# The down projection in seven-product form over pairs of token tiles, with its weight combinations stored ahead

## The chip, the cores and the metric

The kernel runs on one core of one Trainium2 chip. The metric is the device time of one execution in microseconds. Five engines of the core matter here. TensorE (PE in the profile) multiplies 128x128 blocks. VectorE (DVE) and GpSimd (POOL) do elementwise arithmetic. ScalarE (ACT) does activations, copies and casts, and issues some transfers. SyncE (SP) only issues transfers. Each engine takes its own instructions strictly in order and waits on semaphores for the others.

## The reference

Two layers' worth of input, 2048 prompt rows and 8 x 16 sample rows, go through one layer: a normalised input projection, a gated-delta group and a short-convolution group, an output projection, and then the feed-forward block that the change is about. With `D_MODEL` 1024 and `D_FF` 2816 it is

```
h = rmsnorm(x, norm_ffn_pre)
f = (silu(h @ w_gate) * (h @ w_up)) @ w_down
x = x + rmsnorm(f, norm_ffn_post)
```

All tensors are float32. The 2176 rows are 17 tiles of 128 rows, tile 16 being the sample rows. `D_FF` is 22 blocks of 128 (`NF`).

## The kernel before

**Split products.** A matmul operand is a reduced float32 type (`F32R`). To keep precision, each operand is split in two: `hi`, the cast of the value, made by ACT, and `lo`, the value minus `hi`, made by DVE or POOL. A product is then three matmuls: hi x hi, hi x lo, lo x hi.

**Stages.** The program has four stages: the input projection with the two mixers, the output projection (`o_tile`), gate/up, and the down projection.

**Gate/up** (L740 to L893). The tiles are taken in three groups (`FGROUPS`: 6, 6 and 5 tiles); each group runs over all 22 column blocks f. It already has a seven-product form (Winograd's variant of Strassen's scheme): the two rows of blocks are gate and up, the two inner halves are the halves of `D_MODEL`, and the two columns are the halves of the group's tokens. Seven products of half the size take the place of eight. `ffn_load` fetches the group's activations from `hTd`; `ffn_prep` makes the seven combinations of activations and splits them (28 pairs `xh`, `xl`). `gu_weights` makes the seven weight tiles of one column block: in group 0 it loads `rg` and `ru`, forms the four sums S1 to S4 on DVE, splits all seven, and stores the four split sums in DRAM (`fsplit`); in groups 1 and 2 it splits only the three plain quarters and fetches the four stored ones. The tiles `fw` are a ring of 12 (`NWB`). `gate_up` runs the seven products, combines them on DVE, POOL and ACT, and stores the result in `actd`, one DRAM tensor for each group and chunk of column blocks.

**Down** (L896 to L957). The 22 blocks are cut into four chunks (`FCHUNKS`: 6, 6, 5, 5). At the start of a chunk `down_weights` loads each block of `w_dn`, casts it on ACT and splits it on POOL. Then `down_tile` runs for each of the 17 tiles: load the tile's part of `actd`, split it (ACT, DVE), multiply it by the chunk's weights into two PSUM banks of 512 columns, and add these to the tile's accumulator `acc[t]` (ACT copies in the first chunk, DVE adds after that). In the last chunk it also squares, normalises, adds the residual `x2d` and stores `y`.

**Order.** The program is written in loops, but the instructions of each engine are put in order by a scheduler that runs a time model of its own while the kernel is built; within one engine that order is then fixed. So a piece of work written after another can come before it, and work of different loops is interleaved.

## Time and profile before

| | |
|---|---|
| median of 3 runs | 2717.77 us (2716.97 to 2719.88) |
| profiled execution | 2717.92 us, span 2716.1 us |
| granted TensorE clock, mean | 0.98 |
| gate/up, group 0 / seam / group 1 / seam / group 2 | from 1258.6 / 1566.7 / 1614.5 / 1895.0 / 1926.0 us |
| entry to the down projection | 2182.5 to 2222.4 us |
| down projection | 2222.4 to 2707.6 us |
| after the last matmul | 2707.6 to 2716.1 us |
| DMA traffic | 561.03 MB, mean 207 GB/s |

The page of the profile gives busy time by engine, the chain of work that ended last, and groups of instructions (line, engine, operation, output <- inputs, size, count | busy us, mean ns of one | idle time before them and what ended it). A table by windows gives for each stretch the length, each engine's busy time with its number of instructions, the granted clock, the DMA share and GB/s. Matmuls overlap in the record, so what one costs in a dense stretch is the stretch divided by the count, not the mean duration. Waiting for a memory port is inside an instruction's recorded duration; waiting for a semaphore is idle time before it.

### The profile page before, as it was taken

The numbers are of one execution on the slowest core, as the hardware profiler recorded it, in microseconds if no ns is written. First come the engines' busy times: TensorE is split into PE (matmuls) and PEld (weight loads), VectorE is DVE, ScalarE is ACT, GpSimd is POOL, SyncE is SP. The second block draws the span as 40 slices with busy tenths as digits, with TensorE's granted clock in tenths as the row PEclk, the third lists the DMA queues.
The fourth block names the chain that finished last, engine by engine and source line by source line (L and its number), as shares of the span: only waits on it lengthen the run. The fifth ranks groups of instructions, "written<-read, shape, count | busy, mean of one in ns | idle before, by whom it ended". The sixth has DMA issues, their size and how long they took to land.

```text
span 2716.1 us, 41011 instructions
## 1 busy us (share of the span) xinstructions
PE 2586.1 (95%) x15369; PEld 2402.7 (88%) x15369; DVE 1412.3 (52%) x3008; ACT 882.0 (32%) x2013; POOL 686.1 (25%) x601
## 2 busy tenths in 40 slices
PE   5789999999999999998999999999999989999998
PEld 4679989899998997877999989999999978888887
DVE  7877656575675656677655562222522221223366
ACT  3424143151423404343444442223433232211122
POOL 2231000010000101124655563444644440201000
PEclk9889999999999999998999999999999999999999
DMA  8887665656666574767766677777788841212144
GB/s 296 297 300 260 221 219 199 227 187 223 216 211 212 185 232 135 233 220 248 270 238 248 243 239 223 229 227 222 229 268 256 257 170 51 95 46 67 49 149 167
DMA packets 255541, 561.03 MB, mean 207 GB/s; under 512 B 48508, under 2 KB 137280, under 8 KB 233840
## 3 DMA queue, kind: packets, MB, share of 16 engines
q1 hardware_dynamic: 162800, 494.93, 54.6%
q10 hardware_dynamic: 92544, 63.49, 7.4%
q8 instruction: 121, 1.98, 0.3%
q14 instruction: 76, 0.62, 0.1%
HBM read 416.74 MB, written 141.60 MB: 206 GB/s over the span
## 4 chain that ended last, share of the span: by engine, by line
PE 51%; DVE 2%; POOL 1%; DMA 1%; issue 1%; ACT 0%; POOLq 0%; ACTq 0%; DVEq 0%
PE fbank L843 31%; PE ybank L936 18%; PE tbank L708 1%; PE dbank L708 1%; DVE xl L781 1%; DMA dr<-in_w_dn 1%; POOL dl L911 0%; DVE fh L775 0%; DVE fh L772 0%; POOL xl L781 0%; POOL fw L822 0%; PE ftbank L730 0%; DMA fh<-hTd 0%; DMA x2d<-xo 0%; POOL ft L766 0%
## 5 line engine op out<-in xcount | busy, mean ns | idle before, releaser
L843 PE MATMUL fbank<-xh,fw 128*128 128x384 f32 (+1 forms) x3696 | 899.1, 326 | 3.5 <-ACT fw L821 2.0
L131 PE MATMUL dbank<-hi,w 128*128 128x384 f32 (+1 forms) x2688 | 704.7, 341 | 36.2 <-POOL w L292 10.7
L843 PEld LDWEIGHTS fbank<-xh,fw 128*128 128x128 f32 x3696 | 652.3, 188 | 5.5 <-ACT fw L821 2.4
L843 PE MATMUL fbank<-xl,fw 128*128 128x384 f32 (+1 forms) x1848 | 604.0, 327 | 10.2 <-DVE xl L781 10.2
L131 PEld LDWEIGHTS dbank<-hi,w 128*128 128x128 f32 x2688 | 493.5, 196 | 49.2 <-POOL w L292 14.1
L131 PE MATMUL dbank<-lo,w 128*128 128x384 f32 (+1 forms) x1344 | 453.6, 338 | 0.0
L843 PEld LDWEIGHTS fbank<-xl,fw 128*128 128x128 f32 x1848 | 347.7, 188 | 13.2 <-DVE xl L781 13.0
L936 PE MATMUL ybank<-dh,ah 128*128 128x512 f32 x748 | 289.4, 392 | 6.7 <-ACT ah L926 6.7
L936 PE MATMUL ybank<-dh,al 128*128 128x512 f32 x748 | 291.9, 391 | 0.9 <-DVE al L927 0.9
L936 PE MATMUL ybank<-dl,ah 128*128 128x512 f32 x748 | 291.6, 390 | 0.0
L131 PEld LDWEIGHTS dbank<-lo,w 128*128 128x128 f32 x1344 | 264.0, 196 | 2.3 <-issue 0.2
L822 POOL TENSOR_TENSOR fw<-rg,fw 128x512 fp32r<-128x512 f32 x132 | 182.8, 1385 | 238.5 <-ACT fw L821 238.5
L936 PEld LDWEIGHTS ybank<-dh,ah 128*128 128x128 f32 x748 | 141.3, 189 | 36.7 <-ACT ah L926 7.4
L936 PEld LDWEIGHTS ybank<-dh,al 128*128 128x128 f32 x748 | 141.0, 188 | 31.2 <-DVE al L927 2.0
L941 DVE TENSOR_TENSOR acc<-acc,ybank 128x512 f32<-128x512 f32 x102 | 69.9, 685 | 188.8 <-PE ybank L936 188.6
L936 PEld LDWEIGHTS ybank<-dl,ah 128*128 128x128 f32 x748 | 141.0, 189 | 29.4 <-POOL dl L911 0.2
L870 DVE TENSOR_TENSOR u<-m,fbank 128x384 f32<-128x384 f32 (+1 forms) x66 | 35.0, 530 | 238.6 <-PE fbank L843 238.6
L927 DVE TENSOR_TENSOR al<-ar,ah 128x768 fp32r<-128x768 f32 (+1 forms) x68 | 75.1, 1107 | 128.3 <-ACT ah L926 128.3
L821 ACT CAST fw<-rg 128x512 fp32r<-128x512 f32 x132 | 82.3, 624 | 163.9 <-PE fbank L843 155.0
L926 ACT CAST ah<-ar 128x768 fp32r<-128x768 f32 (+1 forms) x68 | 53.2, 785 | 253.1 <-PE ybank L936 251.3
L317 DVE SCALAR_TENSOR_TENSOR acc<-R,cw,acc 128x384 f32<-128x384 f32 (+1 forms) x216 | 129.6, 604 | 1.6
L911 POOL TENSOR_TENSOR dl<-dr,dh 128x1024 fp32r<-128x1024 f32 x22 | 53.6, 2443 | 254.2 <-ACT dh L910 251.7
(292 smaller groups left out, 3560.2 us busy)
## 6 DMA issues: line engine op xcount, KB each, us to landing
w<-wsplit SPq DMA_DIRECT2D x140, 1024.0 KB, 5.0
fw<-fsplit SPq DMA_DIRECT2D x176, 512.0 KB, 4.4
fsplit<-fw SPq DMA_DIRECT2D x88, 512.0 KB, 3.0
rg<-in_w_gu SPq DMA_DIRECT2D x66, 512.0 KB, 4.2
wsplit<-w SPq DMA_DIRECT2D x28, 1024.0 KB, 5.1
actd<-at ACTq DMA_DIRECT2D x44, 384.0 KB, 4.9
wr<-in_w_in SPq DMA_DIRECT2D x56, 256.0 KB, 5.7
ar<-actd SPq DMA_DIRECT2D x34, 384.0 KB, 3.1
```

The costliest lines, as they stand in the source:

```text
L131: T.matmul(ps, l, r, start=(i == 0), stop=(i == n - 1))
L317: V.scalar_tensor_tensor(acc, raw(d), w[:, d:d + 1], acc, op0=ALU.mult, op1=ALU.add)
L708: T.matmul(pss[n], m_[:, j, :], w_[k][:, n * 512:(n + 1) * 512], start=(k == 0 and ci == 0), stop=(k == KD - 1 and ci == 2))
L821: A.copy(w[:, 0], v)
L822: e.tensor_tensor(out=w[:, 1], in0=v, in1=w[:, 0].bitcast(F32), op=ALU.subtract)
L843: T.matmul(ps, w_[:, c], b_[k][:, :hw], start=(first and k == 0 and ci == 0), stop=(k == KH - 1 and ci == 2), skip_group_check=not first)
L870: V.tensor_add(u2, s1, b2)
L911: G.tensor_tensor(out=wl, in0=wr, in1=wh.bitcast(F32), op=ALU.subtract)
L926: A.copy(ah[:, :c * P], ar[:, :c * P])
L927: V.tensor_sub(al[:, :c * P], ar[:, :c * P], ah[:, :c * P].bitcast(F32))
L936: T.matmul(ps[nh], a_[:, q], w_[:, h], start=(kk == 0 and ci == 0), stop=(kk == c - 1 and ci == 2))
L941: V.tensor_add(acc[t][:, h], acc[t][:, h], ps[nh])
```

## The change

**The down projection** takes the seven-product form too. The two block rows are the two tiles of a pair (`down_pair`, 8 pairs), the two inner halves are the two halves of a chunk's column blocks, the two columns are the halves of `D_MODEL`. `FCHUNKS` becomes 4, 4, 4, 4, 6, so that each chunk has two equal halves. Tile 16 has no partner and is done alone (`down_single`) with four of the seven weight tiles. Each pair has four PSUM banks, and seven activation combinations, of which DVE forms four and ACT, DVE and POOL split all; DVE and POOL add the partial results to the accumulators. In the last chunk `finish_tile` ends each tile; its residual add goes to POOL, except for the last two tiles.

**The weight combinations** of the down projection are made once, during gate/up: eleven jobs `down_split`, after columns 1, 4, ... 19 of group 1 and 0, 3, 6, 9 of group 2. A job loads two blocks of `w_dn` on SP, forms four differences on DVE, casts on ACT and splits on POOL into a ring of two tiles `ds`, and stores the seven split tiles in `dsplit`, by transfers that ACT issues. The down stage fetches them into a ring of 23 tiles (`wfetch`): 10 of these (`dr`) take the memory of the jobs' tiles and are filled from column 10 of group 2 on, 13 lie in the down stage's pool.

**Gate/up** stores only two of its four sums (i = 3 and 6). In groups 1 and 2 it loads both halves of `ru` and makes S3 and S1 again, with their splits, on DVE. The pool `fs` of the activations is closed after group 0's preparation, and later groups use the jobs' pool `fd`.

```diff
-FCHUNKS = [range(0, 6), range(6, 12), range(12, 17), range(17, 22)]
+FCHUNKS = [range(0, 4), range(4, 8), range(8, 12), range(12, 16), range(16, 22)]
...
+    wring = {}
+    worder = [(ch, i, q) for ch, c in enumerate(FCHUNKS) for i in range(7) for q in range(len(c) // 2)]
+
+    def wfetch(n):
+        for ch, i, q in worder[:n]:
+            pool, b = (dr, NDR) if len(wring) % NDW < NDR else (dn, NDW - NDR)
+            w = pool.tile([P, 2, 512], F32R, tag="dw", name="dw", bufs=b)
+            nc.sync.dma_start(out=w.bitcast(F32), in_=dsplit[ch][q][:, i])
+            wring[ch, i, q] = w
+        del worder[:n]
...
-            if gi:
-                nc.sync.dma_start(out=a22, in_=w_gu[f, 1].rearrange("p k c -> p (k c)")[:, 512:])
-                s = [None] * 4
-            else:
-                nc.sync.dma_start(out=ru, in_=w_gu[f, 1].rearrange("p k c -> p (k c)"))
-                s = [fb.tile([P, 512], F32, tag=nm, name=nm) for nm in ("sA", "sB", "sC", "sD")]
-                V.tensor_sub(s[2], a11, a21)
-                V.tensor_add(s[0], a21, a22)
+            fload[gi, f] = nc.sync.dma_start(out=ru, in_=w_gu[f, 1].rearrange("p k c -> p (k c)"))
+            s = [None] * 4
+            s[2] = fb.tile([P, 512], F32, tag="sC", name="sC")
+            V.tensor_sub(s[2], a11, a21)
+            s[0] = fb.tile([P, 512], F32, tag="sA", name="sA")
+            V.tensor_add(s[0], a21, a22)
+            if not gi:
...
+        def down_split(ch, q, after):
+            c = len(FCHUNKS[ch]) // 2
+            r1 = fd.tile([P, D], F32, tag="dr", name="dr1", bufs=2)
+            r2 = fd.tile([P, D], F32, tag="dr", name="dr2", bufs=2)
+            with tc.issue_after(after.ins):
+                nc.sync.dma_start(out=r1, in_=w_dn[FCHUNKS[ch][q]])
+                nc.sync.dma_start(out=r2, in_=w_dn[FCHUNKS[ch][c + q]])
+            b11, b12, b21, b22 = r1[:, :512], r1[:, 512:], r2[:, :512], r2[:, 512:]
+            t3 = fd.tile([P, 512], F32, tag="dt3", name="dt3")
+            V.tensor_sub(t3, b22, b12)
+            V.tensor_sub(b12, b12, b11)
+            for i, v in enumerate((b11, t3, b12, b12, b21, b12, b22)):
+                if i == 3:
+                    V.tensor_sub(b12, b22, b12)
+                elif i == 5:
+                    V.tensor_sub(b12, b21, b12)
+                w = fd.tile([P, 2, 512], F32R, tag="ds", name="ds", bufs=2)
+                A.copy(w[:, 0], v)
+                G.tensor_tensor(out=w[:, 1], in0=v, in1=w[:, 0].bitcast(F32), op=ALU.subtract)
+                nc.scalar.dma_start(out=dsplit[ch][q][:, i], in_=w.bitcast(F32))
+
+        djobs = [(ch, q) for ch, c in enumerate(FCHUNKS) for q in range(len(c) // 2)]
+        dwhen = [(1, f) for f in range(1, NF, 3)] + [(2, f) for f in (0, 3, 6, 9)]
...
+        def split(v, e):
+            n = v.shape[-1]
+            a = dn.tile([P, 2, MC * P // 2], F32R, tag="as", name="as", bufs=NDA)
+            A.copy(a[:, 0, :n], v)
+            e.tensor_tensor(out=a[:, 1, :n], in0=v, in1=a[:, 0, :n].bitcast(F32), op=ALU.subtract)
+            return a
...
+        def finish_tile(t):
...
+                V.scalar_tensor_tensor(acc[t][:, h], acc[t][:, h], r, gpo[:, h], op0=ALU.mult, op1=ALU.mult)
+                acc_add(xt[:, h], acc[t][:, h], V if t >= NT - 2 else G)
...
+        def down_pair(ch, t, last):
+            first = ch == 0
+            e = V if last and ch == len(FCHUNKS) - 1 else G
+            c11, c12 = halves(t)
+            c21, c22 = halves(t + 1)
+            a11, a12 = load_act(ch, t)
+            a21, a22 = load_act(ch, t + 1)
+            free = lambda: wfetch(len(FCHUNKS[ch]) // 2 if last else 0)
+            b1, b3, b4, b2 = ybank(), ybank(), ybank(), ybank()
+            product(b1, ch, split(a11, V), 0, True)
+            free()
+            s1 = tmp("s1")
+            A.copy(s1, b1)
+            st = tmp("st")[:, :a11.shape[-1]]
+            V.tensor_add(st, a21, a22)
+            V.tensor_sub(a21, a11, a21)
+            product(b3, ch, split(a21, G), 1, True)
...
+                acc_add(c22, b3)
+            product(b4, ch, split(st, V), 2, True)
+            free()
+            acc_add(c22, b4)
+            V.tensor_sub(st, st, a11)
+            product(b2, ch, split(st, G), 3, True)
+            free()
+            u2 = tmp("u2")
+            V.tensor_add(u2, s1, b2)
+            acc_add(c22, u2, G)
+            product(b1, ch, split(a12, V), 4, False)
...
+                acc_add(c11, b1)
+            product(b3, ch, split(a22, G), 5, False)
...
+                acc_add(c21, b3)
+                acc_add(c21, u2, e)
+            V.tensor_sub(a12, a12, st)
+            product(b4, ch, split(a12, V), 6, False)
...
+                acc_add(c12, b4)
+                acc_add(c12, u2, e)
+            if ch == len(FCHUNKS) - 1:
+                finish_tile(t)
+                finish_tile(t + 1)
```

173 lines of the change are left out of this document (115 added, 58 removed).

## The prediction

> **What bounds the kernel now.** I read the page first, then the chain that ended last, then busy time by stage.
>
> ```profile
> span 2716.1 us, 41011 instructions
> PE 2586.1 (95%) x15369; PEld 2402.7 (88%) x15369; DVE 1412.3 (52%) x3008; ACT 882.0 (32%) x2013; POOL 686.1 (25%) x601
> ```
>
> ```profile
> 2182.45 0.85 POOL m L876
> 2183.29 6.82 issue
> 2190.16 2.35 POOL dl L911
> ...
> 2222.38 485.16 PE ybank L936 x2132
> ```
>
> ```profile
> core 0: us, PE busy (x) PEld busy (x) DVE busy (x) ACT busy (x) POOL busy (x), PEclk, DMA share, GB/s
> ...
> 1566.70:1614.50 47.80, 41.72 (x232) 39.64 (x231) 36.36 (x41) 23.39 (x51) 36.61 (x29) 1.00 0.63 210
> 1614.50:1895.00 280.50, 280.48 (x1618) 280.48 (x1619) 65.94 (x98) 78.18 (x154) 113.14 (x98) 1.00 0.76 232
> 1895.00:1926.00 31.00, 26.29 (x155) 24.60 (x153) 25.29 (x30) 15.71 (x38) 25.24 (x22) 1.00 0.63 200
> 1926.00:2182.50 256.50, 256.42 (x1748) 256.42 (x1749) 69.55 (x111) 80.58 (x170) 115.66 (x105) 1.00 0.80 254
> 2182.50:2222.40 39.90, 32.34 (x144) 26.11 (x142) 9.43 (x8) 14.75 (x19) 21.15 (x10) 0.96 0.45 157
> 2222.40:2707.60 485.20, 485.12 (x2132) 401.19 (x2132) 179.10 (x262) 103.19 (x174) 42.02 (x30) 1.00 0.28 93
> 2707.60:2716.10 8.50, 0.00 (x0) 0.00 (x0) 3.58 (x7) 0.72 (x2) 0.55 (x1) 0.68 0.24 91
> ```
>
> TensorE is busy 95% of the span. The chain's last long piece is 485 us of down-projection matmuls without a gap, and in that stage DVE, ACT and POOL are nearly idle. Gate/up groups 1 and 2 are gapless too. TensorE loses time only at three seams: group 0 to 1 (47.8 - 41.72 = 6.1 us), group 1 to 2 (31.0 - 26.29 = 4.7 us), and into the down projection. All sums stand against the profiled execution: 2717.92 us, a span of 2716.1 and 1.8 around it; the median of three runs, 2717.77, is the same within 0.2 us. A measurement of this kernel tells 0.2%, 5.4 us, from no change.
>
> **Part 1, fewer matmuls.** Before: 17 tiles x 22 column blocks x 2 halves x 3 split terms = 2244 of 512 columns. After: 8 pairs x 7 products x 11 x 3 = 1848, and 4 x 11 x 3 = 132 for tile 16, 1980 together, which the built order confirms. One costs 485.12 / 2132 = 0.2275 us, so 264 fewer give -60.1 us. All of it lay on the path.
>
> **Part 2, entry to the down projection.** Of the 144 matmuls in the 39.9 us window, 2244 - 2132 = 112 are 512 wide (25.5 us) and 32 belong to gate/up at 256.42 / 1748 = 0.1467 us (4.7 us): 9.7 us were lost to loading and splitting weights. After, ten split tiles are already there and tile 16's activations are fetched before gate/up ends, but the first cast stands on ACT behind the last column's SiLU and `actd` issue, as before.
>
> ```profile
> L843 PE MATMUL fbank<-xh,fw x3696: 302/334/689, 1256.8 to 2186.7; 128*128 128x384 f32 x130, 128*128 128x320 f32 x65
> L936 PE MATMUL ybank<-dh,ah x748: 389/389/797, 2191.8 to 2706.7; 128*128 128x512 f32 x187
> ```
>
> From the last gate/up to the first down matmul were 2191.8 - 2186.7 = 5.1 us. I keep that and count 9.7 - 5.1 = -4.6 us (ends: -9.7, and 0 if the four weight tiles that wait for the last gate/up matmul come late). The 22 loads, casts and POOL splits of `w_dn` that go from this stage lay beside matmuls everywhere else and give nothing more; in their place stand 22 loads and 77 stores in groups 1 and 2 (part 4) and 77 fetches.
>
> **Part 3, the two seams between groups.** Prices, group 1's rows first, then group 2's 320-column forms, then the page's:
>
> ```profile
> L822 POOL TENSOR_TENSOR fw<-rg,fw 128x512 fp32r<-128x512 f32 x38 | 49.2, 1294 | 95.0 <-ACT fw L821 95.0
> L871 POOL TENSOR_TENSOR m<-m,m 128x384 f32<-128x384 f32 x19 | 19.2, 1011 | 31.1 <-ACT m L863 31.1
> L875 DVE TENSOR_TENSOR c<-u,fbank 128x384 f32<-128x384 f32 x18 | 10.0, 554 | 63.9 <-PE fbank L843 63.9
> L880 DVE TENSOR_TENSOR at<-c,m 128x384 f32<-128x384 f32 x18 | 10.1, 559 | 2.0 <-DVE c L875 0.4
> L881 DVE TENSOR_TENSOR at<-m,c 128x384 f32<-128x384 f32 x19 | 22.6, 1188 | 12.6 <-ACT c L878 12.6
> ```
>
> ```profile
> L871 POOL TENSOR_TENSOR m<-m,m 128x320 f32<-128x320 f32 x20 | 17.6, 878 | 22.0 <-ACT m L863 20.7 <-ACT m L862 1.3
> L875 DVE TENSOR_TENSOR c<-u,fbank 128x320 f32<-128x320 f32 x21 | 10.2, 488 | 58.5 <-PE fbank L843 58.5
> L878 ACT ACTIVATE c<-c 128x320 f32<-128x320 f32 x21 | 9.8, 468 | 4.5 <-DVE c L877 4.5
> L861 ACT COPY m<-fbank 128x320 f32<-128x320 f32 x20 | 8.5, 427 | 14.8 <-PE fbank L843 14.8
> ```
>
> ```profile
> L821 ACT CAST fw<-rg 128x512 fp32r<-128x512 f32 x132 | 82.3, 624 | 163.9 <-PE fbank L843 155.0
> L941 DVE TENSOR_TENSOR acc<-acc,ybank 128x512 f32<-128x512 f32 x102 | 69.9, 685 | 188.8 <-PE ybank L936 188.6
> L950 DVE SCALAR_TENSOR_TENSOR acc<-acc,f2r,gpo 128x512 f32<-128x512 f32 x34 | 24.0, 748 | 12.3 <-POOL f2r L125 12.3
> L125 POOL TENSOR_TENSOR f2r<-f2m,neghalf 128x1 f32<-128x1 f32 x17 | 9.3, 549 | 209.7 <-DVE f2m L123 209.7
> ```
>
> A DVE add with both inputs in SBUF (L881) takes 1188 ns where POOL works, 559 alone. The timeline of DVE, then of POOL, shows how they share:
>
> ```profile
> 1574.95 1.35 DVE L769 TENSOR_TENSOR fh<-fh 128x384 f32<-128x384 f32 x1 [3.25 <-POOL ft L766]
> 1576.23 1.64 DVE L781 TENSOR_TENSOR xl<-ft,xh 128x384 fp32r<-128x384 f32 x1
> ...
> 1592.72 2.65 DVE L775 TENSOR_TENSOR fh<-fh 128x384 f32<-128x384 f32 x2
> ```
>
> ```profile
> 1574.88 1.01 POOL L871 TENSOR_TENSOR m<-m,m 128x384 f32<-128x384 f32 x1
> 1575.85 1.60 POOL L822 TENSOR_TENSOR fw<-rg,fw 128x512 fp32r<-128x512 f32 x1
> ...
> 1592.56 3.67 POOL L781 TENSOR_TENSOR xl<-fh,xh 128x384 fp32r<-128x384 f32 x3 [0.18 <-ACT xh L780]
> ```
>
> DVE's op issued at 1574.95 ends 0.41 us after POOL's (1575.89), its next 0.42 us after POOL's next (1577.45): they take turns. With both full, 3.67 us held three POOL ops (3.03 alone) and 3.67 / 1.325 = 2.8 DVE ops (1.55 alone): 4.58 us of work in 3.67, a factor of 0.80. I price everything that both do on SBUF at 0.80 of the sum.
>
> At a seam, DVE and POOL split the next group's activations and TensorE waits for them. By the built order, between the first and last of these splits there are added, at 0 to 1: 7 DVE ops (S3 and S1 recomputed and split, and three of the first down job) and 4 POOL `ds` splits: 7 x 0.685 + 4 x 1.294 = 10.0, x 0.80 = 8.0 us. At 1 to 2: 11 DVE ops (7.4 us) and net 8.2 us of POOL: 15.6 x 0.80 = 12.5 us. Together +20.5 us. Ends: 0 (TensorE still has the last column's products to cover it) and 32, if ACT also blocks there: the third `ds` cast waits for the first `dsplit` write to land, and the second product's last cast is queued behind it.
>
> **Part 4, groups 1 and 2 between the seams.** Per column POOL rises from 3 x 1.294 + 2 x 0.878 = 5.6 us to 8.7 (7 `ds` splits over three columns), DVE-on-SBUF to about 4.7: 13.4 x 0.80 = 10.7, under TensorE's 84 x 0.1467 = 12.3 in group 2. ACT: five casts of 0.624, five ops of about 0.44 and a third of 7 casts, 6.8. `fw`'s ring of 12 gives lead, so engines cost nothing here. SP's queue takes two whole loads per job and drops two `fsplit` loads per column. DMA is the tight one: per column 2.1 MB weights, 0.33 `actd` and a third of a job's 4.7 MB are 4.0 MB in 12.3 us, 325 GB/s, where 254 GB/s took a share of 0.80 (318 at full). For the 12 columns with jobs that is 2% over, +3 us (ends 0 and 15, 10% over). The ten `dw` fetches then stand on SP ahead of column 12's loads: 5.2 MB, 16 us, inside the ring's lead.
>
> **Part 5, pairs in chunks 0 to 3.** TensorE needs 42 x 0.2275 = 9.56 us a pair. DVE: 6 PSUM adds at 0.685 and 8 of 256 columns at 0.42 (by the 320, 384 and 512 rows) = 7.5; POOL: 3 splits at 0.74 and 3 adds at 1.294 = 6.1. The shared part is (3.4 + 6.1) x 0.80 = 7.6, so it fits; but DVE waits for turns, half an op for each of POOL's 6 (3 us), which brings it to the edge. I take 0.25 us for 24 pairs, +6 (ends 0 and 24). Fetches (0.5 MB a tile) run in the ring of 23, ahead of use.
>
> **Part 6, last chunk.** TensorE 63 x 0.2275 = 14.33 us a pair. On SBUF: DVE 8 x 0.56 + 4 x 0.748 = 7.5; POOL 3 x 1.01 + 7 x 1.294 (three accumulations, four residual adds) + 2 x 0.549 = 13.2. Together 20.7 x 0.80 = 16.5: 2.2 us over. For 7 pairs +15.5 (the last is relieved by DVE); ends 0 and 35. This is the work that the idle POOL of before is to hide, and it does not quite.
>
> The Trainium skill, "SBUF — State Buffer", section "SBUF: two separate sides", calls this pair of ports an exclusive lock held for the whole instruction. The waits above agree; the full stretch shows 0.80, not 1. By that rule the last chunk would cost 45 us instead of 15.5.
>
> **Tail.** The same chain (add, square, power, scale, add, store), 8.5 us: 0.
>
> **Sum.** -60.1 - 4.6 + 20.5 + 3 + 6 + 15.5 = -19.7, so 2698 us.
>
> **Rivals.**
> All hidden: DVE and POOL stand idle half the time, and the seams' additions serve columns that come later. Then seams cost 5 and the last chunk 5: 2717.9 - 64.7 + 10 = 2663. Against it: at the seam POOL and DVE are already busy 36 of 47.8 us. 0.20.
> Full serialisation (factor 1): seams 25.6, last chunk 45, parts 4 and 5 as above: 2717.9 - 64.7 + 25.6 + 9 + 45 = 2733, slower. For it: the two waits of 0.41; against: the full stretch. 0.12.
> ACT held by its own stores: `ds` has two buffers, so five casts of a job wait for a landing.
>
> ```profile
> fsplit<-fw SPq DMA_DIRECT2D x88, 512.0 KB, 3.0
> ```
>
> ```profile
> 2176.51 0.37 ACTq L883 DMA_DIRECT2D actd<-at  x1
> ```
>
> At 3.0 us it is covered by what ACT does in between. With queues full and 6 us it is not: three columns of group 2 need 16 + 4 (casts of the job) + 3 (its 7 issues at 0.37) + 5 x 4 (waits, beyond some 2 us of cover) = 43 us of ACT against 37, 26 us over four jobs, and 20 at the seams: 2698 + 46 = 2744, slower. It decides from 5 us on. 0.16.
> That the matmuls do not fall is excluded by the order.
>
> **Numbers.** Forecast case 0.52, of it 0.07 within 5.4 us of no change; so are 0.02 of the slow cases. Faster 0.20 + 0.45 = 0.65, same 0.07 + 0.02 = 0.09, slower 0.26. The range runs from the hidden case, 2663, past the serialised one to 2736; what the ACT case holds beyond that, 0.16, is left out.
>
> **What would show it.** 1980 down matmuls at 0.2275; seam windows losing about 14 and 17 us; chunks at about 9.8 us a pair; POOL near full in the last chunk, pairs of 16.5 us; `dsplit` landing under 5 us. Wrong, if TensorE stalls inside groups 1 or 2, if seams lose nothing, or if pairs run at TensorE's pace.

## The result and the profile after

The changed kernel takes 2761.06 us (median of 4 runs, 2759.71 to 2765.10), the kernel before 2717.37 (4 runs, 2715.22 to 2719.88): a ratio of 1.0163, interval 1.0145 to 1.0181. It is slower by 43.7 us, 1.6%, where 2698 had been forecast and the range ended at 2736. The profiled executions have spans of 2757.5 and 2716.1 us, 41.4 apart. From the page of the changed kernel:

```profile
span 2757.5 us, 42084 instructions
...
PE 2571.3 (93%) x15105; PEld 2362.3 (86%) x15105; DVE 1881.1 (68%) x3597; ACT 1013.4 (37%) x2406; POOL 1078.2 (39%) x908
```

The 264 matmuls are gone (15105 for 15369); DVE and POOL work 469 and 392 us more. Busy time by stage of the changed kernel: columns 0 to 2 of group 1, its other columns, columns 0 to 3 of group 2, its other columns, chunk 0, chunks 1 to 3, the last chunk, the tail (columns as in the prediction):

```profile
1586.90:1644.80 57.90, 49.28 (x255) 47.49 (x254) 51.56 (x55) 25.34 (x52) 45.06 (x33) 0.91 0.67 235
1644.80:1936.80 292.00, 282.08 (x1597) 279.39 (x1597) 168.09 (x199) 120.39 (x240) 188.09 (x143) 0.99 0.78 268
1936.80:2003.80 67.00, 56.78 (x339) 53.33 (x338) 59.90 (x67) 32.74 (x73) 55.29 (x43) 0.90 0.63 216
2003.80:2236.60 232.80, 225.20 (x1513) 223.12 (x1512) 125.81 (x166) 91.12 (x188) 130.95 (x104) 0.99 0.72 247
2239.10:2328.50 89.40, 84.96 (x361) 67.39 (x362) 60.03 (x104) 36.50 (x88) 30.06 (x33) 1.00 0.51 181
2328.50:2591.60 263.10, 261.00 (x1082) 199.15 (x1081) 235.36 (x348) 73.78 (x199) 158.55 (x143) 1.00 0.38 134
2591.60:2743.10 151.50, 135.19 (x541) 104.57 (x539) 132.99 (x176) 52.31 (x127) 120.96 (x91) 0.94 0.44 159
2743.10:2757.50 14.40, 0.12 (x1) 0.00 (x0) 9.19 (x16) 1.74 (x6) 3.99 (x4) 0.60 0.39 147
```

Columns 3 to 21 of group 1 and columns 4 to 21 of group 2 in the kernel before:

```profile
1632.70:1909.30 276.60, 276.60 (x1598) 276.60 (x1596) 70.04 (x100) 80.34 (x160) 117.02 (x101) 1.00 0.75 226
1965.10:2186.70 221.60, 221.60 (x1513) 221.60 (x1511) 56.84 (x90) 67.20 (x140) 95.12 (x86) 1.00 0.79 250
```

TensorE had no gap there. Now it has 10 us of gaps in group 1's columns alone, while DVE's busy time there went from 70 to 168 us. In the next table each stage runs from the start of its first matmul to the start of the next stage's (84 matmuls are a column of gate/up).

| stage | before | after | moved | forecast |
|---|---|---|---|---|
| to gate/up's first matmul | 1256.8 | 1259.5 | +2.8 | 0 |
| group 0, columns 0-2 | 47.6 | 50.8 | +3.1 | 0 |
| group 0, columns 3-21 | 276.6 | 276.6 | 0 | 0 |
| group 1, columns 0-2 (seam) | 51.6 | 57.9 | +6.3 | +8 |
| group 1, columns 3-21 | 276.6 | 292.0 | +15.4 | +3 in both groups |
| group 2, columns 0-3 (seam) | 55.8 | 67.0 | +11.2 | +12.5 |
| group 2, columns 4-21 | 221.6 | 232.5 | +10.9 | (above) |
| entry | 5.1 | 2.8 | -2.3 | 0 |
| down projection | 515.3 | 503.7 | -11.6 | -43.2 |
| tail | 9.0 | 14.7 | +5.7 | 0 |

The forecast kept the 5.1 us of the entry and took its 4.6 us from the first matmuls of the down projection, so they stand in that row.

The down projection has its 60.1 us, but 48.5 come back: against 0.2275 us a matmul chunk 0 is 7.4 us over, chunks 1 to 3 are 17.4 over and the last 28.8; the kernel before was 5 over in all.

Where no number of runs is given, a kernel below was run once. How well such rows repeat: kernels with the same order of instructions took 1253.0 to 1265.4 us up to gate/up's first matmul, so the table's first row is scatter, and the single spans below are good to some 6 us. Stages are steadier: two more kernels with the changed kernel's gate/up had 291.0 and 292.5 us in group 1's columns and 235.6 and 233.3 in group 2's. Two kernels with another gate/up, written the same in both (three `ds` tiles, below), had 286.8 and 282.7, and 223.0 and 225.3. A difference of 4 us in one such stage is therefore no evidence.

What a stall is made of can be seen in column 7 of group 1, which took 18.2 us for 14.56. ACT, then DVE:

```profile
1706.50 0.62 ACT L866 CAST ds<-dr 128x512 fp32r<-128x512 f32 x1 [1.98 <-DMA dsplit<-ds]
1709.25 0.33 ACTq L868 DMA_DIRECT2D dsplit<-ds  x1
1709.67 0.62 ACT L866 CAST ds<-dr 128x512 fp32r<-128x512 f32 x1 [2.55 <-POOL ds L867]
1710.20 0.62 ACT L842 CAST fw<-rg 128x512 fp32r<-128x512 f32 x1
1712.57 0.52 ACT L925 ACTIVATE c<-c 128x384 f32<-128x384 f32 x1 [1.76 <-DVE c L924]
...
1714.21 0.48 ACT L908 COPY m<-fbank 128x384 f32<-128x384 f32 x1 [1.11 <-DVE at L928]
```

```profile
1706.57 1.50 DVE L864 TENSOR_TENSOR dr<-dr,dr 128x512 f32<-128x512 f32 x1
1707.99 1.77 DVE L843 TENSOR_TENSOR fw<-sA,fw 128x512 fp32r<-128x512 f32 x1
1709.80 0.69 DVE L830 TENSOR_TENSOR sA<-ru 128x512 f32<-128x512 f32 x1
1710.41 0.55 DVE L922 TENSOR_TENSOR c<-u,fbank 128x384 f32<-128x384 f32 x1
```

TensorE waits for the eviction at 1714.21. That stands on ACT behind two casts of a job, one waiting for a store to land and one for POOL, and behind an activation that waits for DVE; and DVE is late with its combination, because a job's sum and the split of S1 took 1.50 and 1.77 us, where 0.69 is the time alone. No engine is full: they wait for each other.

### The profile page after: what moved, and what is told of

Its sections match the earlier page's. It is cut to its first block, busy times and chain, and to the rows that moved or that the text cites. A ratio compares the mean times of both kernels' runs of the same rounds, so it can differ in the third digit from the quotient of the medians.

```text
span 2757.5 us, 42084 instructions
## 1 busy us (share of the span) xinstructions
PE 2571.3 (93%) x15105; PEld 2362.3 (86%) x15105; DVE 1881.1 (68%) x3597; ACT 1013.4 (37%) x2406; POOL 1078.2 (39%) x908
## 3 DMA queue, kind: packets, MB, share of 16 engines
q1 hardware_dynamic: 157328, 477.63, 50.8%
## 4 chain that ended last, share of the span: by engine, by line
PE 27%; DVE 12%; DMA 10%; POOL 5%; issue 4%; ACT 2%; SPq 0%; ACTq 0%; DVEq 0%; POOLq 0%
PE fbank L890 21%; PE ybank L985 5%; DMA ar<-actd 3%; DMA ru<-in_w_gu 2%; DVE as L977 1%; DMA dr<-in_w_dn 1%; DVE acc L956 1%; POOL fw L843 1%; POOL as L977 1%; DMA dsplit<-ds 1%; DVE fw L843 1%; POOL xr L958 1%; DMA mr<-mixd 1%; POOL acc L958 1%; DVE acc L998 1%
## 5 line engine op out<-in xcount | busy, mean ns | idle before, releaser
L985 PE MATMUL ybank<-dw,as 128*128 128x512 f32 x1980 | 481.3, 401 | 25.3 <-ACT as L976 5.9
L985 PEld LDWEIGHTS ybank<-dw,as 128*128 128x128 f32 x1980 | 371.1, 190 | 135.3 <-ACT as L976 17.2
L958 POOL TENSOR_TENSOR acc<-acc,u 128x512 f32<-128x512 f32 x102 | 149.2, 1463 | 70.8 <-DVE u L1036 62.8
L843 POOL TENSOR_TENSOR fw<-ru,fw 128x512 fp32r<-128x512 f32 x66 | 90.8, 1376 | 108.4 <-ACT fw L842 102.1
L976 ACT CAST as<-ar 128x256 fp32r<-128x256 f32 (+1 forms) x210 | 82.4, 425 | 116.1 <-DVE ar L1051 62.3
L956 DVE TENSOR_TENSOR acc<-acc,ybank 128x512 f32<-128x512 f32 x176 | 118.5, 676 | 2.8 <-PE ybank L985 2.7
L843 DVE TENSOR_TENSOR fw<-sC,fw 128x512 fp32r<-128x512 f32 x66 | 75.7, 1147 | 63.7 <-ACT fw L842 61.3
L867 POOL TENSOR_TENSOR ds<-dr,ds 128x512 fp32r<-128x512 f32 x66 | 96.7, 1465 | 50.7 <-ACT ds L866 50.5
L828 DVE TENSOR_TENSOR sC<-rg,ru 128x512 f32<-128x512 f32 x66 | 69.7, 1056 | 55.5 <-DMA ru<-in_w_gu 52.3
L977 DVE TENSOR_TENSOR as<-ar,as 128x256 fp32r<-128x256 f32 (+1 forms) x130 | 91.3, 705 | 22.2 <-ACT as L976 21.8
```

Source lines behind the costliest of these rows:

```text
L828: V.tensor_sub(s[2], a11, a21)
L843: e.tensor_tensor(out=w[:, 1], in0=v, in1=w[:, 0].bitcast(F32), op=ALU.subtract)
L867: G.tensor_tensor(out=w[:, 1], in0=v, in1=w[:, 0].bitcast(F32), op=ALU.subtract)
L956: V.tensor_add(dst, dst, ps)
L958: G.tensor_tensor(out=dst, in0=dst, in1=ps, op=ALU.add)
L976: A.copy(a[:, 0, :n], v)
```

## The experiments

Kernels that are named here for one edit are the changed kernel with that edit. "Steady columns" are 3 to 21 of group 1 and 4 to 21 of group 2; they lost 15.4 and 10.9 us.

**Without the jobs.**

```diff
-            nc.sync.dma_start(out=w.bitcast(F32), in_=dsplit[ch][q][:, i])
+            nc.sync.dma_start(out=w.bitcast(F32), in_=fsplit[0][:, 3])
...
-            if (gi, f) in dwhen:
+            if False:
                 down_split(*dwhen[gi, f], fload[gi, f + 1])
```

> This kernel leaves the eleven down_split jobs out; every weight tile of the down projection is fetched from one stored gate/up combination instead, so y is not the layer's output. In the changed kernel gate/up lost 49.7 us against the kernel before: 5.9 before its fourth column, 6.3 at the first seam, 15.4 in columns 3 to 21 of group 1, 11.2 at the second seam and 10.9 in columns 4 to 21 of group 2. Theory A (the jobs hold ACT: their casts wait for loads and stores, and ACT's evictions of PSUM queue behind them): without jobs group 1 returns to 276.6 us and group 2's columns to 221.6, and the two seams lose at least 10 of their 17.5 us; the 5.9 us at the start stay. Theory B (S3 and S1, recomputed on DVE in every column, and the shared SBUF path are what costs): 10 us or more stay in the steady columns.

Measured: 2726.0 us, steady columns 276.64 and 221.61, to the hundredth those of the kernel before; the seams lose 2.5 and 2.9. All of the steady loss and 12 us of the seams' 17.5 need the jobs. S3 and S1 recomputed without jobs cost the steady columns nothing, so Theory B falls. Theory A's numbers are met, but a run without jobs does not tell ACT's part in them from DVE's or POOL's. The steady columns of group 1, then of group 2:

```profile
1642.40:1919.00 276.60, 276.60 (x1597) 276.60 (x1596) 123.62 (x177) 103.64 (x204) 126.45 (x102) 1.00 0.54 172
1977.70:2199.30 221.60, 221.60 (x1513) 221.60 (x1512) 109.47 (x154) 82.76 (x172) 106.18 (x86) 1.00 0.58 181
```

**S3 and S1 fetched as before, with the jobs.**

```diff
+            h = slice(512, 1024) if gi else slice(0, 1024)
...
-                    if not gi and i in (3, 6):
+                    if i in (1, 2, 3, 6):
```

(In groups 1 and 2 no sums are made, and only the second half of `ru` is loaded.)

> The split tiles of S3 and S1 are stored in group 0 and fetched in groups 1 and 2 as in the kernel before, in place of recomputing them on DVE; the jobs stay. In the changed kernel DVE stood idle 21 us of 172 in group 1 until a gate/up load landed, because the first of the two sums stands in its order ahead of gate/up's combinations and the jobs' sums, and 23 us more until ACT had cast its tile. Theory R (the recomputation, by these waits in DVE's order, makes the jobs too much): the steady losses of 15.4 and 10.9 us fall under 5 and under 4, and the seams' 17.5 to 13 or less. Theory C (DMA, at a share of 0.76 and 0.86 now, takes 0.8 MB more a column): the losses grow, to 20 us or more in group 2. If neither holds, the jobs' own chain costs it, and the losses stay within 3 us.

Measured: 2723.3 us; steady columns 276.6 and 222.4, the seams 4.2 and 5.9 over. Theory R holds, C falls: group 1's columns run without a gap at a DMA share of 0.97 and 339 GB/s, beside jobs and all:

```profile
1643.30:1920.00 276.70, 276.70 (x1599) 276.70 (x1598) 98.14 (x124) 105.82 (x210) 180.42 (x145) 1.00 0.97 339
```

So it takes both, the jobs and the recomputation. The next runs ask what of them.

**The wait for the load, on DVE.** A ring of three for `ru`.

```diff
-            ru = fb.tile([P, D], F32, tag="ru", name="ru", bufs=2)
+            ru = fb.tile([P, D], F32, tag="ru", name="ru", bufs=3)
```

> One edit: the second gate/up load tile, ru, gets a ring of three instead of two; S3 and S1 are recomputed as in the changed kernel. There DVE stood idle 21 us of 172 in group 1 until ru had landed. Theory R1 (it is this wait, in DVE's order ahead of gate/up's own operations): with ru a column earlier the steady losses of 15.4 and 10.9 us fall under 7 and under 5. Theory R2 (it is the recomputation's work, four operations of 0.7 to 1.4 us a column on the path that POOL shares, with the jobs'): they stay within 4 us.

DVE's waits in group 1's steady columns, in the changed kernel and with the deeper ring (waiting operation, releaser: us in total, times, longest):

```profile
DVE fw L843 <- ACT fw L842: 41.1, 19, 6.8
DVE sC L828 <- DMA ru<-in_w_gu: 28.3, 16, 3.1
...
DVE dt L858 <- DMA dr<-in_w_dn: 9.8, 6, 1.9
```

```profile
DVE fw L843 <- ACT fw L842: 30.7, 15, 3.6
DVE dt L858 <- DMA dr<-in_w_dn: 19.8, 6, 4.3
```

Measured: 2762.2 us; the 28.3 us of waiting are gone, and the columns lose 19.0 and 7.2. R1 falls and R2's bound is met: a wait in an in-order queue, taken away, gave its time to the next wait.

**The load on the path of DVE and POOL, without the jobs' hand-overs.** Seven POOL and four DVE subtractions of 512 columns per job, from `at` into scratch. The ring of `at` is four deep instead of two, and the weights are fetched as in the kernel without jobs:

```diff
-            at = fb.tile([P, 2 * HW], F32, tag="at", name="at", bufs=2)
+            at = fb.tile([P, 2 * HW], F32, tag="at", name="at", bufs=4)
...
-            if (gi, f) in dwhen:
-                down_split(*dwhen[gi, f], fload[gi, f + 1])
+            n = {0: 4, 1: 3}.get((f - 1) % 3 if gi == 1 else f % 3 if gi == 2 and f < 11 else 2, 0)
+            for _ in range(n):
+                z = fd.tile([P, 512], F32R, tag="ds", name="ds", bufs=2)
+                G.tensor_tensor(out=z, in0=at[:, :512], in1=at[:, 128:640], op=ALU.subtract)
+            for _ in range(n // 2 + n % 2):
+                z = fd.tile([P, 512], F32, tag="dt3", name="dt3", bufs=2)
+                V.tensor_sub(z, at[:, :512], at[:, 128:640])
```

> No jobs, and the down projection's weights again fetched from one stored gate/up combination, so y is not the layer's output. In their place POOL does 77 subtractions of 512 columns and DVE 44, four and two, then three and two, after the same columns, from the tile that gate/up has just made into scratch tiles that nobody reads: the jobs' work on the path of DVE and POOL without their loads, casts, stores and hand-overs. Counted at the times that operations take alone, DVE's and POOL's operations on SBUF then fill 0.9 to 0.95 of TensorE's time in columns 3 to 21 of group 1 (0.94 in the changed kernel, which lost 15.4 us there, 0.69 without jobs, which lost nothing). Theory P (the path's load alone does it): group 1's columns lose 8 us or more, and group 2's columns 4 to 21 5 or more. Theory Q (it takes the hand-overs between three engines' queues as well; the load only stretches them): they lose under 4 and under 3.

Measured: 2753.6 us; group 1's columns lose 4.8, group 2's 10.7, the seams 3.1 and 13.2. Theory P is met in group 2 and not in group 1, Theory Q in neither: in group 2 the load alone costs as much as the jobs did, in group 1 a third of it. The jobs' transfers are gone here too (a DMA share of 0.53 in group 1's columns, for 0.78), so the other two thirds are not the hand-overs' for certain; but with S3 and S1 fetched the same transfers, at 0.97, cost nothing.

**Who does the jobs' work.** Splits on DVE, and, in another kernel, casts and stores by POOL:

```diff
-                G.tensor_tensor(out=w[:, 1], in0=v, in1=w[:, 0].bitcast(F32), op=ALU.subtract)
+                V.tensor_sub(w[:, 1], v, w[:, 0].bitcast(F32))
```

> The jobs stay where they are, but the 77 subtractions that split their tiles run on DVE in place of POOL. In the changed kernel a column of group 1 lost 15.4 us in all over the steady part, with DVE at 97 us of work in 172 (68 in 160 without jobs) and its 512-wide SBUF operations at 1.0 to 1.5 us where 0.69 is the time alone. Theory S (POOL's operations and DVE's share one path, so what is taken from POOL comes back on DVE): the steady losses of 15.4 and 10.9 us fall under 9 and under 6, although DVE has 77 operations more. Theory H (the handshake of cast, split and in-place sums, whichever engine splits): they stay within 3 us. Theory W (work of DVE): they grow by 5 us or more.

```diff
-                A.copy(w[:, 0], v)
+                G.tensor_copy(out=w[:, 0], in_=v)
...
-                nc.scalar.dma_start(out=dsplit[ch][q][:, i], in_=w.bitcast(F32))
+                nc.gpsimd.dma_start(out=dsplit[ch][q][:, i], in_=w.bitcast(F32))
```

> The same jobs at the same places, but their 77 casts run on POOL and their 77 stores are issued by POOL, so ACT does none of it. Theory A (ACT's order): the losses of 15.4 and 10.9 us in the steady columns fall under 4 and 4 us although POOL gets 77 casts, about 80 us, more. Theory B (POOL and DVE on one SBUF path): the losses stay or grow, to 20 us or more in group 1. Theory C (DMA at its limit): the losses stay within 3 us of what they were, since the bytes and their times are the same.

Measured: with the splits on DVE 2747.2 us and 9.2 and 6.7 lost, a little short of what S asked (under 9 and 6), but outside H's 3 us and far from W; with the casts on POOL 2796.7 us, 24.4 and 11.5 lost, and an entry of 21.9 us (SP's first fetches wait 24 us for a late job's store). In group 1 that is Theory B's 20 or more, and A and C fall; group 2 moved by 0.6 us. ACT's place in the jobs is not what costs most: freed of them, it waits 104 us for DVE's combinations in group 1. (The second edit also moves the issue of the stores, so its size is not that of the casts alone.)

**The hand-overs of the jobs.** A third `ds` tile; the loads a column sooner; the jobs called in three parts (with a second edit, below):

```diff
-                w = fd.tile([P, 2, 512], F32R, tag="ds", name="ds", bufs=2)
+                w = fd.tile([P, 2, 512], F32R, tag="ds", name="ds", bufs=3)
```

> The ring of ds tiles is three deep instead of two. In the changed kernel ACT waited 22.3 us for dsplit stores to land in group 1 and 18.6 us in columns 3 to 10 of group 2. Theory A1 (the store's landing is what holds ACT): these waits fall by half or more, and the steady columns, which lost 15.4 and 10.9 us, lose under 8 and under 6. Theory A2 (the load of w_dn holds it, 17.3 and 7.9 us of ACT's waits): the loss stays within 3 us of what it was, since the first cast of a job waits as before.

```diff
-                down_split(*dwhen[gi, f], fload[gi, f + 1])
+                down_split(*dwhen[gi, f], fload[gi, f])
```

> The two w_dn loads of a job are ordered behind the gate/up load of the job's own column instead of the next column's, so they are issued one column (14.6 or 12.3 us) sooner. Theory A2: ACT's wait for the load (17.3 us in group 1, 7.9 in columns 3 to 10 of group 2) goes to under 3 us, and the steady columns' losses of 15.4 and 10.9 us fall by half or more. Theory A1: the loss stays within 3 us, because the job's casts then only wait for the store's landing sooner.

```diff
             for i, v in enumerate((b11, t3, b12, b12, b21, b12, b22)):
+                if i in (3, 5):
+                    yield
...
-            nc.sync.dma_start(out=xt, in_=x2d[t])
+            with tc.issue_after(arload[0].ins):
+                nc.sync.dma_start(out=xt, in_=x2d[t])
```

> Two edits in stages that do not meet. First, each job of seven weight tiles is called in three parts, three tiles after its own column and two after each of the next two, in place of all seven at once. Theory A' (the burst of a job, a chain of cast, split and in-place subtraction over three in-order queues, stands ahead of gate/up's own operations): the steady columns' losses of 15.4 and 10.9 us fall under 8 and under 5. Theory C (the amount of work or bytes, not its place): they stay within 3 us. Second, the residual loads xr of the last chunk are ordered behind that chunk's own activation loads; in the changed kernel three of them, 1.5 MB, stood ahead of the second pair's activations at the start of the down projection, where ar loads took 9.9 us to land and chunk 0 lost 7.4 us. If they are what delayed it, chunk 0 loses 3 us or less; if the thirteen dw fetches in front do, it loses 6 or more still.

Measured: with three `ds` tiles 2742.2 us, 10.1 and 1.4 lost, and 3.2 more at the second seam: 26.3 us became 11.6. A1's bounds are met in group 2 and missed by 2 us in group 1; A2 falls. The same gate/up in the kernel with the down edits (below) lost 6.1 and 3.7, 9.8 together. DVE and POOL have the same work as in the changed kernel in both. ACT's largest waits in group 1's columns, in the changed kernel:

```profile
ACT c L925 <- DVE c L924: 59.5, 18, 4.8
ACT ds L866 <- DMA dsplit<-ds: 21.4, 10, 3.6
ACT ds L866 <- DMA dr<-in_w_dn: 17.3, 6, 3.0
```

With three tiles no wait for `dsplit` is left among the largest. With the loads sooner 2772.3 us, 23.9 and 8.6 lost: A2 falls here too, and A1's 3 us do not hold in group 1. The parts (2752.3 us, 13.5 and 9.7 lost) tell nothing: the built order had the seven tiles of a job mostly in two columns, four and three, and moved hardly any of them for the new calls.

**The jobs off the seams.**

```diff
-        dwhen = [(1, f) for f in range(1, NF, 3)] + [(2, f) for f in (0, 3, 6, 9)]
+        dwhen = [(1, f) for f in (4, 7, 10, 12, 14, 16, 18)] + [(2, f) for f in (3, 5, 7, 9)]
```

> The changed kernel with nothing but its jobs moved off the seams (group 1 after columns 4, 7, 10, 12, 14, 16, 18, group 2 after 3, 5, 7, 9). The seams, which lost 6.3 and 11.2 us, should lose what is left without jobs, 2.5 and 2.9, if the operations of the jobs between the splits cost it; if it is the recomputed sums alone, the seams lose 12 or more still. The steady columns lose 26 us or more, as the jobs stand closer.

Measured: 2773.6 us; the first seam loses 3.2, the second 7.5, of it only 1.7 in its first two columns, where no tile of a job is left (10.1 in the changed kernel); the steady columns lose 28.9 and 12.8. Jobs between the splits cost a seam, and standing closer they cost the columns more.

**A common measure.** Count each operation of POOL, and of DVE where no operand is in PSUM, at the time that its form takes while the other engine is quiet (512 columns: 1.28 and 0.68 us; 384: 1.01 and 0.55; 320: 0.88 and 0.49), and divide by TensorE's time, for columns 3 to 21 of group 1:

| kernel | DVE + POOL, us | of 276.6 | lost, us |
|---|---|---|---|
| before | 23.5 + 116.4 | 0.51 | 0 |
| no jobs | 74.2 + 117.3 | 0.69 | 0 |
| S3, S1 fetched | 40.2 + 173.2 | 0.77 | 0 |
| splits on DVE | 119.6 + 114.6 | 0.85 | 9.2 |
| load without hand-overs | 89.9 + 167.9 | 0.93 | 4.8 |
| three `ds` tiles | 90.1 + 170.7 | 0.94 | 10.1 |
| changed kernel | 90.6 + 170.0 | 0.94 | 15.4 |
| three `ru` tiles | 89.2 + 172.2 | 0.94 | 19.0 |
| loads sooner | 89.9 + 174.2 | 0.95 | 23.9 |
| jobs off the seams | 93.2 + 178.7 | 0.98 | 28.9 |
| casts on POOL | 86.8 + 206.2 | 1.06 | 24.4 |

(The last row counts POOL's issues of the stores too, 37 of 0.57 us.) Up to 0.77 nothing is lost, jobs or not, and from 0.85 on every kernel loses. But the load does not set the size: at 0.93 to 0.95 the loss goes from 4.8 us without hand-overs to 23.9, and three `ds` tiles, with the changed kernel's work, took 15 us off the two groups.

Are the two engines then at the limit of what they can do together? In all of group 1's steady columns the changed kernel got through 260.6 us of such work in 292.0, 0.89 us in 1 us. In column 0 of groups 1 and 2, where they split activations side by side, it got through 1.13 and 1.18 (28.3 and 27.5 us long), and the kernel before through 1.20 and 1.18 (21.8 and 18.8 us). In columns 4 to 10 of group 2 it was 0.97, and 1.05 with three `ds` tiles, which lost only 1.4 us there although the work was 1.07 of TensorE's time. So in the steady columns the engines stood below the pace that they reach elsewhere, and waited for each other; that their common path is full there is not shown. These sums overstate the work a little, since consecutive operations overlap in the record: in the kernel before, DVE operations of 0.55 us start 0.47 us apart at 1582.56, 1583.03 and 1583.50.

**The down projection: where the adds run.** `u2`'s adds on DVE; the residual adds on DVE:

```diff
-            acc_add(c22, u2, G)
+            acc_add(c22, u2)
...
-            e = V if last and ch == len(FCHUNKS) - 1 else G
+            e = V
```

> The three adds of u2 in each pair run on DVE in place of POOL, in all chunks. POOL keeps its three splits a pair (and the residual adds of the last chunk). In the changed kernel a pair of chunks 1 to 3 took 9.7 to 11.0 us with DVE at 9.5. Theory S: DVE gains three operations of 0.68 and loses 1.3 us and more of waiting for POOL, 9.5 to 10.3 of work, so the three chunks (263.1 us) stay within 6 us of what they were and the last chunk (151.7) falls to 140 to 147. Theory W: DVE's work rises by its full 2.0 us a pair and the three chunks grow to 275 or more.

```diff
-                acc_add(xt[:, h], acc[t][:, h], V if t >= NT - 2 else G)
+                acc_add(xt[:, h], acc[t][:, h])
```

> All residual adds of the last chunk run on DVE; before, POOL did 30 of 34 at 1.64 us each. In the changed kernel the last chunk took 151.7 us where TensorE needs 122.9, with DVE 73 to 99% and POOL 64 to 93% busy. Theory S (the shared path: POOL's adds slow DVE's SBUF operations, 1.0 us where 0.56 is the time alone): DVE takes four adds of 0.68 a pair but its other operations shrink by about 5 us a pair, and the chunk falls to 130 to 140. Theory W (DVE's own work is the limit): four more operations on an engine at 19 us of 21.7 make it 155 to 165.

DVE's groups in chunks 1 to 3 and POOL's adds there (2330 to 2590 us), in the changed kernel, then DVE's with `u2`'s adds on DVE (count, busy, mean ns, idle before):

```profile
L956 DVE TENSOR_TENSOR acc<-acc,ybank 128x512 f32<-128x512 f32 x123 | 82.8, 676 | 1.6 <-PE ybank L985 1.6
L977 DVE TENSOR_TENSOR as<-ar,as 128x256 fp32r<-128x256 f32 x75 | 50.0, 668 | 4.2 <-ACT as L976 4.2
L1051 DVE TENSOR_TENSOR ar<-ar,st 128x256 f32<-128x256 f32 x24 | 31.5, 1312 | 0.8
L977 DVE TENSOR_TENSOR as<-st,as 128x256 fp32r<-128x256 f32 x24 | 26.4, 1101 | 0.9 <-ACT as L976 0.9
...
L1021 DVE TENSOR_TENSOR st<-ar 128x256 f32<-128x256 f32 x23 | 13.2, 575 | 16.9 <-DMA ar<-actd 16.9
...
L958 POOL TENSOR_TENSOR acc<-acc,u 128x512 f32<-128x512 f32 x69 | 99.5, 1441 | 46.7 <-DVE u L1036 44.9 <-DVE acc L956 0.2
```

```profile
L956 DVE TENSOR_TENSOR acc<-acc,u 128x512 f32<-128x512 f32 x70 | 51.8, 740 | 0.9
L977 DVE TENSOR_TENSOR as<-ar,as 128x256 fp32r<-128x256 f32 x75 | 38.4, 517 | 0.3 <-ACT as L976 0.3
L1051 DVE TENSOR_TENSOR ar<-ar,st 128x256 f32<-128x256 f32 x24 | 16.7, 696 | 0.4
L977 DVE TENSOR_TENSOR as<-st,as 128x256 fp32r<-128x256 f32 x24 | 11.0, 460 | 0.8 <-ACT as L976 0.8
```

Measured: `u2` on DVE 2735.9 us, chunks 1 to 3 251.6 us (263.1) and the last 139.9 (151.7): better than S had it, for DVE was given 70 adds, 51.8 us, and its busy time fell from 235.4 to 226.6. The residual adds on DVE: 2753.8 us, the last chunk 141.0, 1 us above S's range. W falls twice.

**The ring of activation loads, and the loads of `fh`.**

```diff
-            ar = dn.tile([P, MC * P], F32, tag="ar", name="ar", bufs=4)
+            ar = dn.tile([P, MC * P], F32, tag="ar", name="ar", bufs=6)
...
-            if gi + 1 < len(FGROUPS):
-                hs = ffn_load(gi + 1, fd)
             for f in range(NF):
                 gate_up(gi, f, hid)
+                if f == 3 and gi + 1 < len(FGROUPS):
+                    hs = ffn_load(gi + 1, fd)
```

> Two edits in stages that do not meet. First, group 1's eight activation loads (fh) are called after the fourth column of group 0 instead of ahead of its first, so they no longer stand in SP's queue in front of column 1's weights: if that is what cost the 5.9 us up to the fourth column, that column starts within 1.5 us of the kernel before (1304.4), otherwise it stays at about 1310. Second, the ring of activation loads ar in the down projection is six deep instead of four (s1 one deep, xr two deep, st narrower, to make room). In the changed kernel DVE stood idle 1.1 us in pairs 3 to 6 of chunks 1 to 3 until an ar load landed, and these pairs took 10.9 us against 9.7 for the others. Theory D1 (load ring): pairs 3 to 6 fall to 9.7 to 10.0 and the three chunks from 263.1 us together to 250 to 253. Theory D2 (DVE's own work, 9.5 us a pair where POOL shares its path): the chunks lose less than 4 us of it, since DVE is as full without the wait.

Measured: 2743.0 us. (`s1` is one deep, `xr` two deep and `st` narrower, to make room.) Chunks 1 to 3 take 253.3 us, 9.8 less: D1, at the edge of its ranges (pairs 3 to 6 take 9.7 to 10.5 us, counting from 0). For the `fh` loads, SP's issues in the changed kernel:

```profile
1240.89 26.37 SPq L768 DMA_DIRECT2D fh<-hTd  x8
1267.31 0.43 SPq L823 DMA_DIRECT2D rg<-in_w_gu  x1
1267.79 0.44 SPq L825 DMA_DIRECT2D ru<-in_w_gu  x1
```

With it column 1's weights go out at 1243.59 and 1249.15, ahead of the eight `fh`, and columns 0 to 2 take 46.6 us (50.8; before 47.6). The fourth column still starts at 1310.7, not near 1304.4, since the stretch ahead of gate/up came out at 1264.0 in this execution; the 3.1 us are explained, the 2.8 are scatter. The residual loads put back (the second edit of the parts' kernel) took chunk 0 from 7.4 us over to 3.7. As it came out between 3.4 and 12.7 over in kernels without that edit, and 3.3 to 5.5 over in the other three that have it, this is not shown.

**Together.** The down edits with three `ds` tiles; the fetch with the down edits; and that with the jobs off the seams and the residual tiles in halves.

> The edits that helped, together: u2's adds and the residual adds on DVE, the ring of six for the down projection's activations, the residual loads behind the last chunk's activations, and the ring of three for the jobs' ds tiles. If they act on different waits, chunks 1 to 3 take 246 to 251 us together (263.1 in the changed kernel, 245.8 by TensorE's pace), the last chunk 128 to 136 (151.7, by pace 122.9), chunk 0 about 85 and gate/up loses some 32 us in place of 49.7: a span of 2698 to 2712 where the kernel before had 2716. If DVE's own work is by then the limit (it gets 3 operations more a pair, 4 more in the last chunk), chunks 1 to 3 stay at 252 or more and the last at 140 or more.

> S3 and S1 fetched as in the kernel before, and the edits of the down projection (u2's and the residual adds on DVE, ring of six, residual loads behind the last chunk's activations); the ds ring stays two deep. If the two stages do not meet, gate/up ends as with the fetch alone and the down projection takes 463 to 468 us as with its edits: a span of 2685 to 2696, 0.990 to 0.994 of the kernel before's time. If the freed edits meet a common limit (DMA at 0.97 to 0.99 in groups 1 and 2), it stays above 2700.

> As the kernel with fetch and down edits, with the eleven jobs moved off the seams (group 1 after columns 4, 7, 10, 12, 14, 16, 18, group 2 after 3, 5, 7, 9) and the residual tiles as five halves. With the fetch alone the seams lost 10.1 us and without jobs 5.4. If it is the jobs' operations between the splits that cost the seams, they fall to 3 or less together; the steady columns may lose up to 6 us, since jobs stand closer, with DMA at its limit. The tail falls from 18.6 to 14 to 15. The span: 2674 to 2690. If DMA is what holds the closer jobs, it is 2690 or more.

Measured: the first 2710.9 us (the kernel before beside it 2718.8), down projection 463.5. The second 2688.5 (4 runs), 0.9885 of the kernel before's time, interval 0.9867 to 0.9903. The third 2682.1 (4 runs, 2679.0 to 2684.0), **0.9860, interval 0.9845 to 0.9875**, against 2719.1 (7 runs). Its stages from group 1's first columns to the last chunk:

```profile
1589.00:1641.10 52.10, 46.17 (x254) 44.83 (x253) 30.91 (x39) 19.56 (x40) 33.05 (x27) 0.93 0.73 259
1641.10:1917.80 276.70, 276.70 (x1599) 276.70 (x1598) 100.93 (x128) 105.90 (x212) 184.46 (x148) 1.00 0.96 341
1917.80:1976.00 58.20, 52.67 (x338) 51.59 (x337) 35.60 (x47) 23.98 (x52) 41.10 (x36) 0.94 0.73 268
1976.00:2197.60 221.60, 221.60 (x1513) 221.60 (x1512) 66.73 (x102) 78.21 (x164) 128.29 (x110) 1.00 0.96 337
2200.40:2286.00 85.60, 85.58 (x361) 68.90 (x362) 58.73 (x115) 36.51 (x88) 19.34 (x25) 0.98 0.49 174
2286.00:2535.60 249.60, 249.60 (x1081) 202.85 (x1080) 221.28 (x420) 81.60 (x201) 58.30 (x73) 1.00 0.43 151
2535.60:2662.50 126.90, 125.58 (x541) 100.82 (x540) 122.17 (x220) 49.80 (x123) 41.56 (x37) 1.00 0.49 171
```

The seams lose 0.5 and 2.5 us and the columns nothing. The down projection is 11.7 over Part 1's pace, and of that some 4 us are no stall: in chunks 1 to 3 TensorE is busy all 249.6 us, so 1080 matmuls take 0.231 us each there, for 0.2275 in the kernel before; why is not shown. In gate/up, then, the edits take away all but 3.0 us of the loss in the seams and columns.

## Why the prediction was wrong

**The step that failed** is in Part 4: "13.4 x 0.80 = 10.7, under TensorE's 84 x 0.1467 = 12.3 in group 2", and from it "`fw`'s ring of 12 gives lead, so engines cost nothing here." It took work that fits into a column on average for work that costs nothing. The runs showed 26.3 us of loss in these columns, for 3 forecast. They go to zero without the jobs, and to 0.8 us with S3 and S1 fetched, so it takes both. And with work that differs by 2% or less from the changed kernel's they come out at 10 to 32 us, by the depth of one ring or the time of a load. What the step left out, as column 7 and the third `ds` tile show, is that the jobs' casts, splits and stores stand in the same in-order queues as gate/up's evictions, so that a wait in one queue is handed on to the others.

- **Part 1** was right in the count: 1980 matmuls, 60.1 us at the old pace. The new pace is up to 1.6% slower (0.231 us in chunks 1 to 3 of the last kernel above).
- **Part 2** (-4.6) came out at about zero. The entry fell to 2.8 us, but the wait went to the first pairs, and chunk 0 is 7.4 over.
- **Part 3** (+20.5) was near, 17.5; of it the jobs make 12 (without them 2.5 and 2.9 are lost). The factor of 0.80 is not far off here: 1.13 to 1.20 us of work in 1 us is 0.88 to 0.83.
- **Part 4** (+3, ends 0 and 15): besides the step above, the 0.80 does not carry over from the seam. Columns 0 to 10 of group 2, seam and all, got through 168.2 us of work in 164.1, which is a factor of 1 / 1.03 = 0.97, waits included; at that factor 13.4 us are 13.0, over the 12.3. And DMA, priced as the tight one, was not: 341 GB/s went beside a TensorE without a gap.
- **Part 5** (+6, ends 0 and 24) was 17.4: 12 of it go with the adds on DVE, 10 with the ring of six (they overlap). The wait of DVE for `ar` had no term.
- **Part 6** (+15.5, ends 0 and 35) was 28.8; the mechanism was right and the size off. In pairs 3 to 6 POOL has 53.8 us and DVE 32.5 of work at its times alone, 86.3 in 78.3 us, so a factor of 0.91 in place of 0.80. The 20.7 us of Part 6 are then 18.8 a pair, and pairs 2 to 7 took 18.9 on average. As the factor is read from these very pairs, this confirms the 20.7 and nothing more.
- **The tail** (0) took 5.7 more: the last pairs' residual work is still in DVE's queue when TensorE ends. **The start** (0) took 3.1: `fh`'s loads, whose new pool let them stand ahead of column 1's weights in SP's queue, were not counted.

The prediction also reads DVE as nearly idle in the old down projection; its own row has DVE busy for 179 of 485 us.

The rival of full serialisation, with its 2733, came nearer by luck. Its terms were further off than the forecast's, 25.6 for the seams' 17.5 and 45 for the last chunk's 28.8, and it left Part 4 as it was. The page that the prediction names for it, the Trainium skill's "SBUF — State Buffer", section "SBUF: two separate sides", lists DVE operations with two SBUF inputs among those that take the lock. Here DVE's adds from PSUM, which have one, kept 676 ns while POOL was busy for 159 of 263 us; the rows with two went from 460 and 517 ns to 1101 and 668 ns when POOL had `u2`'s adds as well. Whether the two engines exclude each other wholly is not settled by the sums above, which reach 1.20 us of work in 1 us but count overlapping records.

The rival of ACT held by its stores was half right: those waits were there, 21.4 us in group 1's columns, and the deeper ring took 15 us off the columns. But the landing was 3.0 us, under its point of 5, and ACT freed of the jobs did not help where POOL got them.

What stays open: in group 1, how much of the hand-overs' part is ACT's, POOL's or DVE's order. The deeper `ds` ring brought the loss there to 10.1 and 6.1 us in two kernels, near the 4.8 of the load alone; the other waits, taken away one at a time, were followed by another.

## What to carry to other kernels

Price work for DVE and POOL in one sum, each operation at its time alone, and compare the sum with TensorE's time stage by stage: in group 1 nothing was lost up to 0.77 of it, and from 0.85 on TensorE stalled. Above that, look at the queues and not at the average: which of gate/up's operations stands behind which wait of the side work, and how deep the rings between them are. One more buffer took 15 us off, with the same work. An add of two SBUF tiles was better on DVE than on POOL, where both serve the same deadline: it took 0.74 us there for 1.44, and DVE as a whole got faster. A refetch that DMA has room for can be cheaper than recomputing: here by 36 us of span.

## What the runs showed of the hardware

Stalls cost more than their length, by the granted clock. TensorE in two stretches of the same length, in and behind the second seam of the changed kernel:

```profile
1943.80:1957.50 13.70, 9.66 (x33) 8.86 (x34) 13.70 (x14) 5.22 (x12) 13.70 (x11) 0.50 0.09 35
1960.00:1973.70 13.70, 13.35 (x84) 12.26 (x84) 12.99 (x16) 7.30 (x17) 8.99 (x7) 1.00 0.79 271
```

The first has 51 matmuls fewer; its 4.0 idle us are 27 of them at 0.147 us, the rest is the clock at 0.50. Such spells at half clock, of 3.4, 6.8 and 13.7 us, follow gaps of 1.8 to 4.4 us, but not every gap: group 1's steady columns have five of 1.5 to 2.1 us, and two spells, after gaps of 1.8 and 2.1. There are 34 us of them in groups 1 and 2 of the changed kernel, 17 in its last chunk; the kernel before has 6.8 us of them from group 1 to TensorE's last matmul. The prediction had no term for it. The Trainium skill, "TensorE: Matmul & The Clock Gate", Part 1, states half the clock after an idle window of about 3.4 us. The lengths of the spells, 3.4 us and twice and four times that, agree; but here gaps shorter than 3.4 us were enough.
